# Expert lists of 96 places, weights split a whole unit at a time, and final rows scaled by three engines

## The chip, the core and the metric

The kernel runs on one core of a Trainium2 chip. Its engines run side by side, each through its own queue in order: PE (TensorE) multiplies matrices, DVE (VectorE), ACT (ScalarE) and POOL (GpSimd) work on elements, and SP starts transfers (ACT and POOL can too). The metric is the device time of one execution in microseconds (us).

## The reference, cut to what matters

A layer of a decoder: attention, cross-attention, and then a mixture of 16 experts over 512 tokens of width 1024; the change lies in the mixture and in the norm behind it. Each token takes two experts of one group.

```
    u = _rmsnorm(h, norm_ffn)                       # 512 x 1024
    expert_id, weights = two best experts of the best group of each token
    for e in range(16):
        hidden = silu(u @ w_gate[e]) * (u @ w_up[e])    # 1024 -> 256
        y = y + gate[:, e:e + 1] * (hidden @ w_down[e]) # 256 -> 1024
    h = h + y
    return _rmsnorm(h, norm_final)
```

With these inputs the experts are chosen by 44 to 95 tokens each (counted from the reference's routing).

## The kernel before

The expert stage runs over the experts e = 0 to 15. An expert's tokens stand in a list of CAP = 128 places; POOL gathers their rows into `xe` (128 x 1024), two experts ahead. PE transposes `xe` in eight 128 x 128 blocks (L130); ACT rounds a transposed half to `xh` in the matmul's short type (fp32r) and DVE subtracts that to get the rest, `xl` (L132). The weights come by SP's queue in units of 256 KB pairs, six an expert: c0 to c3 hold 256 rows of gate and up each ([128, 2, 512], 1024 elements a partition), d0 and d1 128 rows of down each. The transfers are far ahead of their use.

`esplit` makes two fp32r tiles of weights: ACT casts them to `wh` (L732), DVE subtracts to `wl` (L733). It works on half a unit, [128, 512], and turns through eight half slots (four tiles of two halves). A product of two split numbers is three matmuls (`mm3`, L137 to L139): x high by w high, x high by w low, x low by w high. The weights are the moving operand with 512 columns; the tokens are the stationary one. Per expert that makes 24 gate/up matmuls into `gu` and 9 into `dn`; the last quarter of down is one fp32 matmul of two passes (L1273), which reads `w` itself. In between stand `sg` (ACT's Silu of `gu`, L1240), DVE's product (L1242), two transposes of it (L1249), and `hh`, `hl`, `hf` from them (L1253 to L1255).

A cast overwrites a slot that an earlier cast filled, so it waits for the last matmul on the slot's old contents. In program order the split calls of an expert are c0 to c3, d0, d1; half of d1 goes through `esplit`. A scheduler puts the instructions into each engine's queue; on ACT the casts of an expert's c1 to c3 stand behind the product of the expert before (`issue_after(W["hid"])`), while the cast of c0 stands ahead of that expert's `sg`.

ACT scales `dn` by the routing weights into `y`, half by half (L1287), and SP stores `y` to a table `Y` (CAP rows an expert). For e = 14 and 15 the combination is done by matmuls with 0/1 matrices (`combine`, L1217). When expert 14 comes, POOL issues eight gathers that add rows of `Y` to `HO` (L1293), two for each of the four token tiles t, and behind them the load of the final norm's gain `g_fin` (L1303). The end ("combine") adds the matmuls' part to `HO` (L1312), squares it on ACT (L1313), takes a reciprocal root in a few small steps (L102 to L110), multiplies the rows by it and `g_fin` on DVE (L1320, two halves a tile), and stores (L1322). Tokens beyond CAP places are treated behind a branch (`overflow`).

## Time and profile before

| | us |
|---|---|
| median of 3 runs (lowest to highest) | 654.46 (653.68 to 654.64) |
| own time of the profiled execution | 653.75 |
| its span | 652.1 |
| PE busy | 609.8 (94%) |
| DVE busy | 460.8 (71%) |
| ACT busy | 375.6 (58%) |
| POOL busy | 56.8 (9%) |

The busy times are sums over the span, which holds stages with different limits. Matmuls are pipelined: one starts about 0.23 us after the other and ends some 0.39 us after its own start, so that what PE can do in a stretch is read from the distances of starts. The profiled execution took 0.7 us less than the median of the runs.

### The profile page before, as it was taken

What the parts mean: (1) busy time and instruction counts of PE and PEld (TensorE: products, weight loads), DVE (VectorE), ACT (ScalarE), POOL (GpSimd) and SP (SyncE); (2) the same over time, 40 slices, a digit from 0 to 9 for tenths busy, and PEclk for the clock granted to TensorE, in tenths of its full rate; (3) what the DMA queues carried; (4) which work ended last, traced back from release to release, by engine and by line L of the source; (5) the groups of instructions that cost most, each with busy time, mean ns of one, the idle gap of its engine ahead of it and who ended that gap; (6) DMA issues with size and microseconds to landing.
All of it is one profiled execution on the core that took longest, in us unless ns stands there. A gap on an engine that the chain in (4) does not pass through costs nothing.

```text
span 652.1 us, 10038 instructions
## 1 busy us (share of the span) xinstructions
PE 609.8 (94%) x3435; PEld 496.6 (76%) x3436; DVE 460.8 (71%) x943; ACT 375.6 (58%) x754; POOL 56.8 (9%) x87
## 2 busy tenths in 40 slices
PE   3999999999999989999999999999999999999970
PEld 2988777888786888888988898777677777777740
DVE  4843798843698996746933574458889999998944
ACT  5632567742576776415622453423388989989741
POOL 2000000000000010000000003000341101100530
PEclk9999999999999999999999999999999999999995
DMA  8545748026766446550643223984999999999593
GB/s 280 175 129 129 193 100 211 22 61 157 162 153 162 110 133 193 173 181 0 185 140 96 68 68 102 370 305 143 299 284 383 387 384 382 383 386 359 111 209 137
DMA packets 105464, 128.86 MB, mean 198 GB/s; under 512 B 8440, under 2 KB 82224, under 8 KB 105408
## 3 DMA queue, kind: packets, MB, share of 16 engines
q1 hardware_dynamic: 101088, 114.40, 55.9%
q0 software_dynamic: 4320, 13.77, 7.8%
q8 instruction: 28, 0.46, 0.3%
q14 instruction: 28, 0.23, 0.1%
HBM read 103.96 MB, written 11.56 MB: 177 GB/s over the span
## 4 chain that ended last, share of the span: by engine, by line
PE 75%; DVE 8%; DMA 7%; ACT 5%; issue 2%; POOL 1%; SPq 0%; DVEq 0%; ACTq 0%; POOLq 0%
PE pj L137 6%; PE pj L139 6%; PE pj L138 6%; PE gu L137 4%; PE pja L137 4%; PE gu L138 4%; PE gu L139 4%; PE pja L138 4%; PE pja L139 4%; PE tr L130 3%; PE pjb L138 3%; PE pjb L137 3%; PE pjb L139 3%; PE o L315 2%; PE dn L137 2%
## 5 line engine op out<-in xcount | busy, mean ns | idle before, releaser
L91 DVE TENSOR_TENSOR wl<-w,wh 128x1024 fp32r<-128x1024 f32 (+1 forms) x64 | 78.0, 1221 | 77.0 <-ACT wh L90 76.5
L90 ACT CAST wh<-w 128x1024 fp32r<-128x1024 f32 (+1 forms) x64 | 67.2, 1050 | 101.4 <-PE pj L138 33.1
L733 DVE TENSOR_TENSOR wl<-w,wh 128x512 fp32r<-128x512 f32 x168 | 108.4, 685 | 5.6 <-ACT wh L732 4.8
L732 ACT CAST wh<-w 128x512 fp32r<-128x512 f32 x168 | 96.6, 621 | 12.8 <-PE gu L139 9.8
L138 PE MATMUL pj<-ul,wh 128*128 128x512 f32 x128 | 51.6, 403 | 0.0
L137 PE MATMUL pj<-uh,wh 128*128 128x512 f32 x128 | 51.3, 401 | 0.0
L139 PE MATMUL pj<-uh,wl 128*128 128x512 f32 x128 | 51.2, 400 | 0.0
L137 PE MATMUL gu<-wh,xh 128*128 128x512 f32 x120 | 48.5, 404 | 0.2 <-ACT xh L132 0.2
L139 PE MATMUL gu<-wh,xl 128*128 128x512 f32 x120 | 47.6, 397 | 0.0
L138 PE MATMUL gu<-wl,xh 128*128 128x512 f32 x120 | 47.1, 393 | 0.0
L137 PE MATMUL pj<-wh,uh 128*128 128x256 f32 (+1 forms) x128 | 37.5, 293 | 2.2 <-ACT uh L132 2.2
L139 PE MATMUL pj<-wh,ul 128*128 128x256 f32 (+1 forms) x128 | 37.5, 293 | 0.0
L138 PE MATMUL pj<-wl,uh 128*128 128x256 f32 (+1 forms) x128 | 37.3, 292 | 0.0
L137 PE MATMUL pja<-wh,fmh 128*128 128x512 f32 x80 | 32.5, 406 | 0.0
L138 PE MATMUL pja<-wl,fmh 128*128 128x512 f32 x80 | 31.9, 399 | 0.0
L139 PE MATMUL pja<-wh,fml 128*128 128x512 f32 x80 | 31.8, 397 | 0.0
L137 PEld LDWEIGHTS pj<-uh,wh 128*128 128x128 f32 x128 | 24.1, 188 | 5.1 <-issue 0.2
L372 ACT ACTIVATE p<-lg,nm 128x512 f32<-128x512 f32 (+3 forms) x32 | 16.9, 527 | 19.0 <-DVE nm L370 18.7
L139 PEld LDWEIGHTS pj<-uh,wl 128*128 128x128 f32 x128 | 24.1, 188 | 4.8
L138 PEld LDWEIGHTS pj<-ul,wh 128*128 128x128 f32 x128 | 24.1, 188 | 4.7
L137 PEld LDWEIGHTS pj<-wh,uh 128*128 128x128 f32 x128 | 25.1, 196 | 3.0 <-ACT uh L132 2.8
L139 PEld LDWEIGHTS gu<-wh,xl 128*128 128x128 f32 x120 | 22.5, 188 | 5.3 <-issue 0.2
(356 smaller groups left out, 1618.9 us busy)
## 6 DMA issues: line engine op xcount, KB each, us to landing
w<-in_w_exp_gate_dram SPq DMA_DIRECT2D x64, 256.0 KB, 7.7
w<-in_w_exp_up_dram SPq DMA_DIRECT2D x64, 256.0 KB, 7.7
w<-in_w_exp_down_dram SPq DMA_DIRECT2D x32, 512.0 KB, 7.6
w<-in_w_in_dram SPq DMA_DIRECT2D x24, 512.0 KB, 4.6
w<-in_w_xkv_dram SPq DMA_DIRECT2D x16, 512.0 KB, 4.2
Y<-y SPq DMA_DIRECT2D x14, 512.0 KB, 8.6
KH<-th SPq DMA_DIRECT2D x32, 128.0 KB, 2.3
w<-in_w_out_dram SPq DMA_DIRECT2D x8, 512.0 KB, 5.7
```

Of the source, the lines that this page charges most:

```text
L90: nc.scalar.copy(h, raw)
L91: nc.vector.tensor_sub(l, raw, h)
L130: nc.tensor.transpose(pt[:, j, :], src[:, k * 128:(k + 1) * 128], ident)
L137: nc.tensor.matmul(o, lh, rh, start=start, stop=False)
L138: nc.tensor.matmul(o, lh, rl, start=False, stop=False)
L139: nc.tensor.matmul(o, ll, rh, start=False, stop=stop)
L315: nc.tensor.matmul(o[hh * HD:(hh + 1) * HD, i * 128:(i + w) * 128], V[:, s, vcol + hh * HD:vcol + (hh + 1) * HD], pTs[hh][:, at:at + w, :] ...
L372: nc.scalar.activation(p_[:, cs], lg[:, cs], AF.Exp, bias=nm, scale=1.0, accum_out=sm)
L732: nc.scalar.copy(h, raw)
L733: nc.vector.tensor_sub(l, raw, h)
```

## The change

Five things are edited. (1) CAP becomes 96: `xe`, `xh`, `hh`, `y` and the rows of `Y` shrink to 96 rows or columns; a transpose makes 96 columns, and matmuls with the tokens as the stationary operand use 96 of its columns, while the moving operand stays at 512. The overflow branch goes on in rounds of MORE = 128. (2) `esplit` takes a whole unit, [128, 1024], in one cast and one subtraction, and draws a tile from the rings `wh` and `wl`, four tiles each, for every call; d1 uses half of its tile. (3) The PSUM pool of `dn` has two tiles of two banks where it had four of one bank; `y` is scaled by one instruction over 1024 elements. (4) `g_fin` is loaded by SP's queue while expert 14 is issued. (5) In the end ACT squares the whole row in one instruction (not for the last tile); POOL (DVE in the last tile) multiplies the second half by `g_fin`, DVE scales the first half, ACT scales the second half by the reciprocal root.

```diff
--- before.py
+++ after.py
...
-CAP = 128
+CAP = 96
+MORE = 128
...
     NEP, NEP2 = 19, 6
...
     def esplit(raw):
-        if not halves:
-            for kind in ("wh", "wl"):
-                tiles = [wtile(kind, [2, 512], F32R) for _ in range(4)]
-                halves.append(itertools.cycle([t[:, i, :] for t in tiles for i in range(2)]))
-        h, l = (next(x) for x in halves)
-        nc.scalar.copy(h, raw)
-        nc.vector.tensor_sub(l, raw, h)
-        return h, l
+        h, l = (wtile(kind, [2, 512], F32R) for kind in ("wh", "wl"))
+        if raw.shape[-1] == 512:
+            raw = raw.unsqueeze(1) if len(raw.shape) == 2 else raw
+        else:
+            raw = raw.rearrange("p a (n c) -> p (a n) c", n=2)
+        n = raw.shape[1]
+        nc.scalar.copy(h[:, :n], raw)
+        nc.vector.tensor_sub(l[:, :n], raw, h[:, :n])
+        return [(h[:, i, :], l[:, i, :]) for i in range(n)]
...
-        xe = xp.tile([128, D], F32, name="xe", bufs=2)
-        at = idx[:, e:e + 1] if e < FIRST else lists[:, e, 0:1]
...
-    dnp = pool(ps3, "dnp", bufs=4, space=PSUM)
+    dnp = pool(ps3, "dnp", bufs=2, space=PSUM)
...
+            x.append([xp.tile([128, 4, CAP], F32R, name=n, bufs=3) for n in ("xh", "xl")])
...
+            for j in range(4):
+                k = half * 4 + j
+                nc.tensor.transpose(pt[:, j, :CAP], xes[e][:, k * 128:(k + 1) * 128], ident[:CAP, :CAP])
+            nc.scalar.copy(x[-1][0], pt[:, :, :CAP])
+            nc.vector.tensor_sub(x[-1][1], pt[:, :, :CAP], x[-1][0])
...
-        gu = gup.tile([128, 2 * FF], F32, name="gu")
+        gu = gup.tile([128, 2 * FF], F32, name="gu")[:CAP]
...
-                parts = []
-                for kk in range(2):
-                    with ExitStack() as then:
-                        if e > 1 and 2 <= c * 2 + kk < 8:
-                            then.enter_context(tc.issue_after(W["hid"].ins))
-                        parts.append(esplit(raws[n][:, kk, :]))
+                if e > 1 and c > 0:
+                    after.enter_context(tc.issue_after(W["hid"].ins))
+                parts = esplit(raws[n])
...
-        parts = [esplit(raws[n][:, 0, nh * 512:nh * 512 + 512]) for nh in range(2)]
-        part1 = esplit(raws[n + 1][:, 0, 0:512])
+        parts = esplit(raws[n])
+        part1 = esplit(raws[n + 1][:, 0, 0:512])[0]
...
-            y = xp.tile([128, D], F32, name="y", bufs=3)
-        dps = []
+            y = xp.tile([CAP, D], F32, name="y", bufs=3)
+        dp = dnp.tile([128, 2, 512], F32, name="dn")[:CAP]
...
-            dp = dnp.tile([128, 512], F32, name="dn")
...
+            mm3(dp[:, nh, :], (hh[:, 0, :], hl[:, 0, :]), parts[nh], True, False)
...
-                    for nh in range(2):
-                        nc.scalar.activation(y[:, nh * 512:nh * 512 + 512], dps[nh], AF.Copy, scale=wof(n))
+                    nc.scalar.activation(y, dp.rearrange("p n c -> p (n c)"), AF.Copy, scale=wof(n))
                 nc.sync.dma_start(Y[n * CAP:(n + 1) * CAP, :], y)
...
+            g_fin = etile([D])
+            nc.sync.dma_start(g_fin, a["norm_final"].partition_broadcast(128))
...
     mark("combine")
-    g_fin = etile([D])
-    nc.gpsimd.dma_start(g_fin, a["norm_final"].partition_broadcast(128))
...
     for t in range(NT):
+        last = t == NT - 1
...
+        cps = spread if t == 0 else dnp.tile([128, 2, 512], F32, name="dn")
+        for nh, cs in enumerate(halves):
...
+            nc.vector.tensor_add(row[:, cs], cp, row[:, cs])
+            if last:
+                nc.scalar.activation(junk[:, nh, :], row[:, cs], AF.Square, accum_out=ss[:, nh:nh + 1])
         st = small.tile([128, 1], F32, name="ss")
-        nc.vector.tensor_add(st, ss[:, 0:1], ss[:, 1:2])
+        if last:
+            nc.vector.tensor_add(st, ss[:, 0:1], ss[:, 1:2])
+        else:
+            nc.scalar.activation(junk.rearrange("p a b -> p (a b)"), row, AF.Square, accum_out=st)
...
+        ot = etile([2, 512])
+        (nc.vector if last else nc.gpsimd).tensor_mul(ot[:, 1, :], row[:, halves[1]], g_fin[:, halves[1]])
         r = rstd_of(st, D)
-        ot = etile([2, 512])
-        for nh in range(2):
-            cs = slice(nh * 512, nh * 512 + 512)
-            nc.vector.scalar_tensor_tensor(ot[:, nh, :], HO[:, t, cs], r, g_fin[:, cs],
-                                           op0=OP.mult, op1=OP.mult)
+        nc.vector.scalar_tensor_tensor(ot[:, 0, :], row[:, halves[0]], r, g_fin[:, halves[0]],
+                                       op0=OP.mult, op1=OP.mult)
+        nc.scalar.activation(ot[:, 1, :], ot[:, 1, :], AF.Copy, scale=r)
+        for nh, cs in enumerate(halves):
```

How the rows stand in the queues now is shown at three places.

PE around the end of expert e's gate/up matmuls, before. `gu` are the accumulators; L137, L138, L139 are the three matmuls of `mm3`; L1249 is the first transpose of the hidden product.

```order
L137 MATMUL gu<-wh,xh 128x512 [waits Activation_49]
L138 MATMUL gu<-wl,xh 128x512 [waits DVE_49]
L139 MATMUL gu<-wh,xl 128x512
L137 MATMUL gu<-wh,xh 128x512 [waits Activation_49]
L138 MATMUL gu<-wl,xh 128x512 [waits DVE_49]
L139 MATMUL gu<-wh,xl 128x512
L137 MATMUL gu<-wh,xh 128x512 [waits Activation_49]
L138 MATMUL gu<-wl,xh 128x512 [waits DVE_49]
L139 MATMUL gu<-wh,xl 128x512
L137 MATMUL gu<-wh,xh 128x512 [waits Activation_49]
L138 MATMUL gu<-wl,xh 128x512 [waits DVE_49]
L1249 MATMUL tr<-ident,sg 128x128 [waits DVE_49]
```
The first six rows are c3, the next five c0 of the next expert. Each half slot has its own pair of waits: one matmul waits for ACT's cast, the next for DVE's subtraction. The same place after the change (lines have moved by one or two); the first two rows are the last of c2, the next six are c3, the three after them c0 of the next expert.

```order
L139 MATMUL gu<-wl,xh 96x512
L140 MATMUL gu<-wh,xl 96x512
L138 MATMUL gu<-wh,xh 96x512 [waits Activation_49]
L139 MATMUL gu<-wl,xh 96x512 [waits DVE_49]
L140 MATMUL gu<-wh,xl 96x512
L138 MATMUL gu<-wh,xh 96x512
L139 MATMUL gu<-wl,xh 96x512
L140 MATMUL gu<-wh,xl 96x512
L138 MATMUL gu<-wh,xh 96x512 [waits Activation_49]
L139 MATMUL gu<-wl,xh 96x512 [waits DVE_49]
L140 MATMUL gu<-wh,xl 96x512
L1251 MATMUL tr<-ident,sg 128x96 [waits DVE_49]
```
There is one pair of waits to six matmuls, and three matmuls of the next c0 stand ahead of the transposes where five stood.

ACT over the same part of an expert, before, up to `sg`:

```order
L732 CAST wh<-w 128x512 [waits PE_49]
L1287 ACTIVATE y<-dn,held 128x512 [waits DMAHW1_49,PE_49]
L732 CAST wh<-w 128x512 [waits DMAHW7_49,DMAHW6_49,PE_49]
L1287 ACTIVATE y<-dn,held 128x512 [waits PE_49]
L732 CAST wh<-w 128x512
L732 CAST wh<-w 128x512 [waits DVE_49,DMAHW2_49,PE_49,Activation_49]
L132 CAST xh<-tr 128x512 [waits PE_49]
L732 CAST wh<-w 128x512 [waits DMAHW3_49,DVE_49,DMAHW4_49,PE_49,Activation_49]
L732 CAST wh<-w 128x512 [waits DVE_49,PE_49,Activation_49]
L732 CAST wh<-w 128x512 [waits DMAHW5_49,DMAHW6_49,DVE_49,PE_49]
L732 CAST wh<-w 128x512 [waits DVE_49,PE_49]
L1240 ACTIVATE sg<-gu 128x256 [waits PE_49]
```
and after: `hh` and `y` of expert e - 1, between them c2, c3 and d0 of e, then d1's half (512) of e, c0 of e + 1 and `sg` of e:

```order
L1255 CAST hh<-tr 128x192 [waits PE_49]
L1181 CAST xh<-tr 128x384 [waits PE_49]
L731 CAST wh<-w 128x1024 [waits DMAHW4_49,DMAHW5_49,DVE_49,PE_49]
L731 CAST wh<-w 128x1024 [waits DMAHW7_49,DMAHW6_49,PE_49]
L731 CAST wh<-w 128x1024 [waits DMAHW0_49,PE_49]
L1286 ACTIVATE y<-dn,held 96x1024 [waits DMAHW5_49,PE_49]
L1181 CAST xh<-tr 128x384 [waits PE_49]
L731 CAST wh<-w 128x512 [waits DMAHW1_49,DVE_49,PE_49]
L731 CAST wh<-w 128x1024 [waits DMAHW2_49,DMAHW3_49,DVE_49,PE_49]
L1242 ACTIVATE sg<-gu 96x256 [waits PE_49]
L731 CAST wh<-w 128x1024 [waits DMAHW6_49,DMAHW4_49,DVE_49]
```
Where there were single casts with `y` in two halves between them, three casts of 1024 stand in a row ahead of the whole `y`; the cast of the next expert's c0 waits for PE and stands directly ahead of `sg`. The count in that wait is that of the last matmul on this expert's c2, whose tile c0 takes over (four tiles, and c0 is the fourth call after c2); before, the two casts of c0 waited for matmuls 12 and 9 ahead of the last one of `gu`, now it is the seventh from the end, six ahead of the last. Of the three casts in a row, the first waits for c0's last matmul, the second for the last one on d1, the third for the last one on d0 of the expert before.

DVE at the end of the program, after the change: `ss` are sums of squares, `rv`, `rt`, `rr` the steps of the reciprocal root, L1314 is the last addition to `HO`, L1325 and L1327 are the multiplication by `g_fin` and the scaling of a half.

```order
L1314 TENSOR_TENSOR HO<-dn,HO 128x512 [waits PE_49]
L111 SCALAR_TENSOR_TENSOR rr_6866<-rt_6865,ry_6864 128x1 [waits DVE_49]
L1325 TENSOR_TENSOR w<-HO,w 128x512 [waits DVE_49]
L1327 SCALAR_TENSOR_TENSOR w<-HO,rr_6866,w 128x512 [waits DVE_49]
L107 SCALAR_TENSOR_TENSOR rt_6894<-ry_6893,rv_6892 128x1 [waits Activation_49]
L1319 TENSOR_TENSOR ss<-ssf 128x1 [waits Activation_49]
L111 SCALAR_TENSOR_TENSOR rr_6895<-rt_6894,ry_6893 128x1 [waits DVE_49]
L105 TENSOR_SCALAR rv_6923<-ss 128x1 [waits DVE_49]
L1327 SCALAR_TENSOR_TENSOR w<-HO,rr_6895,w 128x512 [waits DVE_49]
L107 SCALAR_TENSOR_TENSOR rt_6925<-ry_6924,rv_6923 128x1 [waits DVE_49,Activation_49]
L111 SCALAR_TENSOR_TENSOR rr_6926<-rt_6925,ry_6924 128x1 [waits DVE_49]
L1327 SCALAR_TENSOR_TENSOR w<-HO,rr_6926,w 128x512 [waits DVE_49]
```
Before the change there stood, behind its last addition (L1312):

```order
L1320 SCALAR_TENSOR_TENSOR w<-HO,rr_6875,w 128x512 [waits DVE_49]
L1320 SCALAR_TENSOR_TENSOR w<-HO,rr_6875,w 128x512
L106 SCALAR_TENSOR_TENSOR rt_6905<-ry_6904,rv_6903 128x1 [waits DVE_49,Activation_49]
L1315 TENSOR_TENSOR ss<-ssf 128x1 [waits Activation_49]
L110 SCALAR_TENSOR_TENSOR rr_6906<-rt_6905,ry_6904 128x1 [waits DVE_49]
L104 TENSOR_SCALAR rv_6934<-ss 128x1 [waits DVE_49]
L1320 SCALAR_TENSOR_TENSOR w<-HO,rr_6906,w 128x512 [waits DVE_49]
L1320 SCALAR_TENSOR_TENSOR w<-HO,rr_6906,w 128x512
L106 SCALAR_TENSOR_TENSOR rt_6936<-ry_6935,rv_6934 128x1 [waits DVE_49,Activation_49]
L110 SCALAR_TENSOR_TENSOR rr_6937<-rt_6936,ry_6935 128x1 [waits DVE_49]
L1320 SCALAR_TENSOR_TENSOR w<-HO,rr_6937,w 128x512 [waits DVE_49]
L1320 SCALAR_TENSOR_TENSOR w<-HO,rr_6937,w 128x512
```
Behind the last addition stand one L1325 and the first halves of tiles 1 to 3 (three rows of L1327), where six rows of L1320 stood.

## Rows read from the trace of the kernel before

**Rows 1.** Busy time of the engines, granted TensorE clock and DMA by stretch

```profile
core 0: us, PE busy (x) PEld busy (x) DVE busy (x) ACT busy (x) POOL busy (x), PEclk, DMA share, GB/s
500.00:520.00 20.00, 19.95 (x93) 15.28 (x92) 18.55 (x39) 17.99 (x35) 2.28 (x2) 1.00 1.06 381
606.00:610.00 4.00, 4.00 (x20) 3.26 (x19) 3.71 (x7) 3.98 (x9) 0.00 (x0) 1.00 0.32 131
634.00:638.00 4.00, 0.45 (x2) 0.03 (x1) 2.87 (x11) 2.41 (x10) 0.00 (x0) 1.00 0.44 149
```

**Rows 2.** Timeline of ACT, five of its instructions (start, duration, idle time before and releaser)

```profile
482.49 0.38 ACT L1240 ACTIVATE sg<-gu 128x256 f32<-128x256 f32 x1
...
492.36 0.39 ACT L1240 ACTIVATE sg<-gu 128x256 f32<-128x256 f32 x1
...
600.52 0.38 ACT L1240 ACTIVATE sg<-gu 128x256 f32<-128x256 f32 x1
...
603.77 1.14 ACT L732 CAST wh<-w 128x512 fp32r<-128x512 f32 x2 [0.85 <-PE gu L139]
...
605.91 0.69 ACT L1287 ACTIVATE y<-dn,held 128x512 f32<-128x512 f32 x1
```

**Rows 3.** Timeline of PE in expert 13, from the input transposes to the down projection

```profile
601.70 0.60 PE L130 MATMUL tr<-ident,xe 128*128 128x128 f32 x4
602.32 0.50 PE L137 MATMUL dn<-wh,hh 128*128 128x512 f32 x1
602.66 0.39 PE L138 MATMUL dn<-wl,hh 128*128 128x512 f32 x1
602.89 0.39 PE L137 MATMUL dn<-wh,hh 128*128 128x512 f32 x1
...
603.35 0.39 PE L139 MATMUL gu<-wh,xl 128*128 128x512 f32 x1
...
604.72 1.02 PE L1273 MATMUL dn<-w,hf 128*128 128x512 f32 x2
605.58 0.60 PE L130 MATMUL tr<-ident,xe 128*128 128x128 f32 x4
```

**Rows 4.** Instructions grouped by line and shape: count, busy us, mean ns, idle before

```profile
L732 ACT CAST wh<-w 128x512 fp32r<-128x512 f32 x168 | 96.6, 621 | 12.8 <-PE gu L139 9.8 <-PE dn L139 2.3 <-PE pja L139 0.3
L90 ACT CAST wh<-w 128x1024 fp32r<-128x1024 f32 x62 | 65.0, 1049 | 101.4 <-PE pj L138 33.1 <-PE pjb L139 19.5 <-PE pja L138 11.9
L733 DVE TENSOR_TENSOR wl<-w,wh 128x512 fp32r<-128x512 f32 x168 | 108.4, 685 | 5.6 <-ACT wh L732 4.8 <-PE gu L138 0.4
L91 DVE TENSOR_TENSOR wl<-w,wh 128x1024 fp32r<-128x1024 f32 x62 | 75.5, 1220 | 76.7 <-ACT wh L90 76.3
```

**Rows 5.** Timeline of PE at 253 us: matmuls with one moving column

```profile
253.36 1.05 PE L548 MATMUL lg<-one,sq 128*128 128x1 f32 x8
```

**Rows 6.** Timelines of SP and POOL from the last early store to the last load

```profile
606.63 0.32 SPq L1288 DMA_DIRECT2D Y<-y  x1
...
610.08 1.61 POOL L1293 DMA_INDIRECT HO<-Y,slot  x1 [22.15 <-DVE wl L733]
...
627.24 1.55 POOL L1293 DMA_INDIRECT HO<-Y,slot  x1 [3.04 <-DMA HO<-Y,slot]
628.21 1.22 POOL L1303 DMA_DIRECT2D w<-in_norm_final_dram  x1
```

**Rows 7.** Timelines of DVE and of SP after the last gather

```profile
636.57 0.69 DVE L1312 TENSOR_TENSOR HO<-dn,HO 128x512 f32<-128x512 f32 x1 [0.89 <-DMA HO<-Y,slot]
...
637.50 0.21 DVE L106 SCALAR_TENSOR_TENSOR rt<-ry,rv 128x1 f32<-128x1 f32 x1
637.84 1.41 DVE L1320 SCALAR_TENSOR_TENSOR w<-HO,rr,w 128x512 f32<-128x512 f32 x2
...
643.44 1.41 DVE L1320 SCALAR_TENSOR_TENSOR w<-HO,rr,w 128x512 f32<-128x512 f32 x2
...
644.22 1.09 SPq L1322 DMA_DIRECT2D out_dram<-w  x2
```

More of the change, by code (lines that the diff above doesn't have):

```diff
@@ L771, in layer @@
     nc.gpsimd.dma_start(Y[LATE * CAP:, :].rearrange("o (p c) -> (o p) c", p=128), zero8)
-    zeroi = rt.tile([128, NE, 2], I32, name="zeroi")
+    zeroi = rt.tile([CAP, NE, 2], I32, name="zeroi")
     nc.gpsimd.memset(zeroi, 0)
@@ L813, in layer @@
     nc.gpsimd.memset(picks[:, 1:5, :], 2.0)
-    iop = rp.tile([128, CAP], BF, name="iop")
-    nc.gpsimd.iota(iop, pattern=[[1, CAP]], base=1, channel_multiplier=0,
+    iop = rp.tile([128, 128], BF, name="iop")
+    nc.gpsimd.iota(iop, pattern=[[1, 128]], base=1, channel_multiplier=0,
                    allow_small_or_imprecise_dtypes=True)
@@ L1037, in layer @@
     xp = pool(c3, "xp", side="right")
-    xf = xp.tile([128, KT, 128], F32, name="y", bufs=3)
+    xf = xp.tile([128, KT, CAP], F32, name="y", bufs=3)
     for half in range(2):
         ks = slice(half * 4, half * 4 + 4)
-        W["xf"] = nc.vector.tensor_mul(xf[:, ks, :], xs[half],
-                                       gT[:, ks].unsqueeze(2).to_broadcast([128, 4, 128]))
+        W["xf"] = nc.vector.tensor_mul(xf[:, ks, :], xs[half][:, :, :CAP],
+                                       gT[:, ks].unsqueeze(2).to_broadcast([128, 4, CAP]))
     ps2.close()
     def overflow():
-        Y2 = dram.tile([NE * 3 * CAP, D], F32, name="Y2")
+        rounds = -(-(S - CAP) // MORE)
+        Y2 = dram.tile([NE * rounds * MORE, D], F32, name="Y2")
         P2 = dram.tile([NE * 128, NT], F32, name="P2")
@@ L1064, in overflow @@
                 nc.vector.tensor_scalar(of, pv, -float(CAP), 0.0, op0=OP.add, op1=OP.max)
-                nc.vector.scalar_tensor_tensor(of, ev, 3.0 * CAP, of, op0=OP.mult, op1=OP.add)
+                nc.vector.scalar_tensor_tensor(of, ev, float(rounds * MORE), of, op0=OP.mult, op1=OP.add)
                 oi = xo.tile([128, NT], I32, name=f"oslot{n}")
@@ L1074, in overflow @@
                 nc.sync.dma_start(pe, P2[ds(e * 128, 128), :])
-                for r in range(3):
+                for r in range(rounds):
                     n_e = nc.values_load(cnti[0:1, ds(e, 1)], min_val=0, max_val=S)
-                    rows = Y2[ds(e * 3 * CAP + r * CAP, CAP), :]
-                    with tc.If(n_e > CAP * (r + 1)) as more:
-                        ior = xo.tile([128, CAP], F32, name="ior")
-                        nc.vector.tensor_scalar(ior, iop, float(CAP * (r + 1)), None, op0=OP.add)
+                    rows = Y2[ds(e * rounds * MORE + r * MORE, MORE), :]
+                    with tc.If(n_e > CAP + MORE * r) as more:
+                        ior = xo.tile([128, MORE], F32, name="ior")
+                        nc.vector.tensor_scalar(ior, iop, float(CAP + MORE * r), None, op0=OP.add)
                         ips = ps.tile([128, 2], F32, name="ips", bufs=1)
                         for t in range(NT):
-                            oh = xo.tile([128, CAP], BF, name="ooh", bufs=2)
+                            oh = xo.tile([128, MORE], BF, name="ooh", bufs=2)
                             nc.vector.tensor_scalar(oh, ior, pe[:, t:t + 1], None, op0=OP.is_equal)
@@ L1175, in head @@
         for half in range(2):
-            x.append([xp.tile([128, 4, 128], F32R, name=n, bufs=3) for n in ("xh", "xl")])
-            to_fm(trp, xes[e][:, half * 512:half * 512 + 512], *x[-1], 0, nk=4)
+            x.append([xp.tile([128, 4, CAP], F32R, name=n, bufs=3) for n in ("xh", "xl")])
+            pt = trp.tile([128, 4, 128], F32, name="tr")
+            for j in range(4):
[3 more added lines that the diff above has]
+            nc.vector.tensor_sub(x[-1][1], pt[:, :, :CAP], x[-1][0])
         if e + 2 < NE:
@@ L1216, in combine @@
         for part in range(2):
-            nc.tensor.matmul(cp, P[:, n, t, :], ylate[n][part][:, nh, :], start=n == 0 and part == 0,
+            nc.tensor.matmul(cp, P[:CAP, n, t, :], ylate[n][part][:CAP, nh, :], start=n == 0 and part == 0,
                              stop=n == NE - LATE - 1 and part == 1)
@@ L1243, in layer @@
         if e == NE - 1:
[L1244 removed]
+            spread = dnp.tile([128, 2, 512], F32, name="dn")
             for nh in range(2):
[L1246 removed]
+                combine(spread[:, nh, :], 0, nh, 0)
         pt = trp.tile([128, 4, 128], F32, name="tr")
         for f in range(2):
[L1249 to L1255 removed]
+            nc.tensor.transpose(pt[:, f, :CAP], hid[:, f * 128:(f + 1) * 128], ident[:CAP, :CAP])
+        hh = xp.tile([128, 2, CAP], F32R, name="hh", bufs=1)
+        hl = xp.tile([128, 2, CAP], F32R, name="hl", bufs=1)
+        hf = xp.tile([128, CAP], F32, name="hf", bufs=1)
+        W["last"] = nc.scalar.copy(hh, pt[:, 0:2, :CAP])
+        nc.vector.tensor_copy(hf, pt[:, 1, :CAP])
+        nc.vector.tensor_sub(hl, pt[:, 0:2, :CAP], hh)
         n = 6 * e + 4
[L1257 to L1258 removed]
+        parts = esplit(raws[n])
+        part1 = esplit(raws[n + 1][:, 0, 0:512])[0]
         late = e >= LATE
```

58 lines of the change are left out of this document (23 added, 35 removed).

## The prediction

> **What bounds the kernel now.** First the stretches. In a full stretch of the expert stage PE is busy 19.95 of 20 us at a granted clock of 1.00, DVE 18.55, ACT 17.99; the weights come at 381 GB/s [rows 1]. Is PE or the weights the bound? At 606 to 610 us, with two experts to go, the DMA share has fallen to 0.32 while the work goes on [rows 1]: the transfers had run ahead, and PE sets the pace. ACT's timeline gives that pace: `sg` starts at 492.36 (e = 2) and 600.52 (e = 13), 108.16 us for 11 experts, **9.83 each**; the interval before was 9.87 [rows 2].
>
> Second, what one expert costs PE, from its timeline [rows 3]. Matmuls of 512 columns start .23 apart (602.66, 602.89) and end .39 after their start. Four transposes last .60 together, the end of the last included; with an end of .16 (.39 - .23) they take (.60 - .16)/4 = .11 each. The fp32 matmul takes 605.58 - 604.72 = .86. So 33 x .23 + .86 + 10 x .11 = 9.55. The rest, .28, is one wait: the transposes of 601.70 are done with issuing at 602.14, `dn` begins at 602.32 (.18), and after that pause the next start is .34 behind instead of .23 (.1).
>
> Third, the end [rows 6, 7]. `y` of expert 13 is finished at 605.91 + .69 = 606.60, stored from 606.63; 3.45 us later POOL starts the first of eight gathers, the eighth at 627.24, and behind them `g_fin`. The last gather lets DVE add at 636.57; multiplications by `g_fin` (L1320) start at 637.84, and the last of the two stores listed at 644.22 is issued at 644.98 (644.22 + 1.09 - .32 for one issue, [rows 6]). From 636.57 that is 8.4; 652.1 - 644.98 = 7.1 behind it stay. So the end of the kernel hangs on the `y` of expert 13, then on the gathers, then on DVE.
>
> **The cast of c0 becomes a loop through PE, ACT and DVE.** Let z be the start of the last matmul on c2 of expert e. It ends at z + .39, ACT hears of it .04 later (603.35 + .39 = 603.74, cast at 603.77 [rows 2, 3]) and casts the whole unit in 1.05, DVE then subtracts in 1.22 [rows 4]. With .04 to .05 a hand-over that is z + .43, z + 1.48, z + 1.52, z + 2.74, and PE's second matmul on the next c0, the one that reads `wl`, can start at z + 2.79. PE has until then only the six matmuls of c3 and the first of c0: it reaches that matmul at z + .23 x 8 = z + 1.84. **It stalls .95**, and the start after a pause costs another .1. What queues behind it: the rest of c0, the transposes of `sg`, `hh`, the down projection, so all of the next expert, whose c2 ends the loop again. The old wait goes: one more gate/up matmul (.23) now stands between the transposes and `dn`, and DVE's product with `sg` and ACT's `hh` are made during and right behind the stall. So 9.55 + .95 + .10 = **10.60** an expert, +.77 on 9.83. Before, the casts of c0 were free 12 and 9 matmuls ahead of the end of `gu`, and worked on 512 in .62 and .685 [rows 4]: the same sum, .39 + .04 + .62 + .04 + .685 + .05 = 1.83 after a release 12 matmuls (2.76) ahead, is hidden. From e = 1 to e = 13 there are 12 intervals: **+9.2** (11, if the first is still covered by early loads: +8.5). If the old .28 stays beside the stall, +3.4 more; that is the upper end.
>
> Does the larger instruction pay elsewhere? Two casts of 512 in a row take 1.14 [rows 2], one of 1024 takes 1.05: ACT gains .09 a unit. This is time on an engine that PE doesn't wait for, but at c0. The Trainium skill, "Perfetto Trace Analysis", section "Optimizing Scalar/DVE Operations", says that grouping into larger operations helps where the engine is saturated, and that where ScalarE or VectorE are not saturated but make bubbles on another engine, breaking instructions up can let work finish sooner. By the first sentence the sum would fall by 5 x .09 an expert on ACT, by the second it rises as above; the rows show ACT at 17.99 of 20, and the second carries.
>
> **96 columns give PE nothing.** The moving operand stays at 512, so the 33 matmuls stay at .23. A transpose holds `xe` as stationary operand (128 columns, now of 96 rows) and moves an identity of 96 columns instead of 128. Eight matmuls with one moving column take 1.05 together, (1.05 - .16)/8 = .11 each [rows 5], as much as a transpose with 128: the moving columns do not set it. I take 0; what fewer rows could give is a rival below. The gathers of `xe` and the stores of `Y` get a quarter smaller; both lie beside PE, but for the last store: 128 KB less at 381 GB/s, **-.3**.
>
> **`y` of expert 13.** It starts the end. Before: 606.60 - 600.52 = 6.08 behind `sg` [rows 2]. After: `sg` starts .04 behind the end of c3's last matmul, at z + 6 x .23 + .39 + .04 = z + 1.81, so the stall ends at sg + .98. Then two matmuls of c0 (.33 + .23), six transposes (.66) and one matmul (.23): `dn` begins at sg + 2.43. Twelve matmuls in a row, of which three are gate/up, take 2.76; the ninth, the last one on d1, ends at sg + 2.43 + 8 x .23 + .39 = 4.66. ACT may cast c3 then: 4.70, and d0 behind it, each at a distance of about .96 (1.05 less the overlap of .09, two casts of .62 starting .52 apart in 1.14); only then, at 6.62, comes `y` with 1024 elements, 1.11 (1.05 x .69/.62 is 1.17, 1.05 + .07 is 1.12). It ends at sg + 7.73: **+1.65**. Here the casts ahead of it, not the down projection (whose last matmul ends at 2.43 + 2.76 + 1.02 = 6.21), are late.
>
> **Gathers and end.** The eight gathers are the same rows of 4 KB and the same waits on each other: 0. `g_fin` leaves POOL's queue, where it stood behind all of them and was the last thing that the scaling waited for (637.84), and goes to SP's, behind the store of `Y`, with nothing behind it until the stores of the end: it lands some 15 us early. So tile 0 is scaled ahead of the last gather; but on DVE the additions, and the steps of tiles 1 and 2, come in turn with the rest. From the last gather G, in DVE's order: the rest of tile 2's addition .69, tile 3's first half .69, then the wait for PE, whose next four matmuls need the tile of two banks that the addition frees (.33 + 2 x .23 + .39 and hand-overs: 1.25), its addition .69, L1325 .69, L1327 of tile 1, 2 and 3 at .71 each (1.41 for two [rows 7]), between the last two the small steps of tile 3's root (two of .21 [rows 7] and one on ACT about as long: .65), two issues .38: 7.2, and some eight hand-overs of .04 make 7.5 to 7.6 where 8.4 stood: **-.9**. Its bounds: 0, if PE's matmuls at G run at half the clock (it stays 1.00 in 634 to 638 with PE busy .45 of 4 us [rows 1]); and -3.3, if nothing of tiles 1 and 2 were left at G (.69 + 1.25 + .69, a square of about .62 as ACT's cast of 512, .65, .71, .38: 5.0, with hand-overs 5.1). POOL's multiplication of 512 has no row; DVE's is .69, and even at 2 us it lies beside the gathers, which take 26.5 us for eight (610.08 to 636.57).
>
> **Sum.** 9.2 + 1.65 - .3 - .9 = +9.65; 653.75 + 9.65 = 663.4 for an execution like the profiled one, which is .7 below the median of the runs: **664**. A difference under 0.2%, about 1.3 us, is what a measurement of this kernel can't tell from none.
>
> **Rivals.** (B) *ACT becomes the bound.* ACT has 2 us of 20 free [rows 1]; if the cast of c0 does not start at its release because `y` or d1's half stand late ahead of it (.5 an expert), the loop is 11.1: 12 x .5 = +6 on top, 670. For it speaks the row of three casts. Against it: `y` ends at sg + 7.73, `xh` and d1's half bring ACT to about sg + 8.75 (.62 each, less the overlaps), and the release comes at sg + 10.60 - 1.81 + .43 = sg + 9.22, so that .5 is free; from there on each .1 more on ACT costs 1.2 us. (C) *Transposes get cheaper with 96 rows.* 10 x .11 x 32/128 = .27 an expert: 12 x .27 = 3.3 less, 660.8. Rows 5 say that the load of the stationary operand sets their .11, but there it had 128 rows. The Trainium skill, "TensorE: Matmul & The Clock Gate", section "LDWEIGHTS (loading the stationary operand)", says that a load's time goes by the columns and not by the contraction, so that 96 rows of 128 columns would cost the same; the trace before has no load of fewer rows to agree or not. (D) *Faster: no stall.* From 1.84 - .43 - .09 = 1.32 downwards for cast and subtraction together the stall is gone; then PE runs through at 9.55 with no pause of .28 either: 12 x -.28 = -3.4, `y` +.7 (the three casts stay, .95 of the 1.65 goes), store -.3, end -.9: -3.9, so 650.5. The same comes out if the tile that c0 takes is one that stood free 12 matmuls earlier. Against it: 1.05 and 1.22 are means over 62 instructions each, and the count in the wait. (E) *A list over 96.* With 95 places at most the branch is not taken; if a place more were counted, the branch's rounds would run, over 680.
>
> **How the numbers follow.** Forecast .77 (662 to 667: 11 intervals, or the old .28 beside the stall), B .08, C .06, D .08, E .01. 664 is the forecast's. Range 660 to 669: it takes in C, and of B the lower part; D and E stay outside. Faster by over 0.2% is D but for its weak cases, .06; those, a stall hidden in part, are within 0.2%: .02; slower are the rest, .92.
>
> **What would show it.** In the changed trace: `sg` 10.6 apart; a wait of about .95 of PE on DVE's `wl` (L732) once an expert, behind one matmul on `wh`; ACT's cast of c0 idle before on PE `gu`; `y` of expert 13 at sg + 7.7; first L1327 ahead of the last gather; about 7.5 us from there to the last issue. It is wrong if PE's starts run through c0 at .23, if transposes of 96 take less than .11, if the cast of c0 does not wait for PE, or if `g_fin` is late on SP.

## The result and the profile after

The changed kernel takes **664.26 us** (median of 4 runs, 663.41 to 666.26) beside 654.55 (4 runs, 653.68 to 655.54) of the kernel before on the same chip: a ratio of 1.0162 [1.0145, 1.018], slower. The forecast was 664.0. Its profiled execution took 666.26, the longest of the four, with a span of 664.6, so the two profiles lie 12.5 apart where the medians lie 9.7 apart. The readings below are from the profiles.

The page's first part gives busy us, share of the span and count of each engine. No engine but PE is near the whole span, and over 500 to 520 us PE too is busy only 18.45 of 20 us, where it was 19.95 [rows 1].

```profile
PE 612.6 (92%) x3435; PEld 481.4 (72%) x3436; DVE 451.5 (68%) x861; ACT 365.7 (55%) x662; POOL 60.3 (9%) x89
```

ACT's timeline (start, duration, idle time before and its releaser) answers to [rows 2]: `sg` of experts 1, 2 and 13, the cast of c0 ahead of the last one, and `y` of expert 13.

```profile
483.95 0.38 ACT L1242 ACTIVATE sg<-gu 96x256 f32<-96x256 f32 x1 [0.34 <-PE gu L140]
494.38 0.38 ACT L1242 ACTIVATE sg<-gu 96x256 f32<-96x256 f32 x1 [0.34 <-PE gu L140]
...
607.62 1.05 ACT L731 CAST wh<-w 128x1024 fp32r<-128x1024 f32 x1 [0.53 <-PE gu L140]
...
609.00 0.38 ACT L1242 ACTIVATE sg<-gu 96x256 f32<-96x256 f32 x1 [0.34 <-PE gu L140]
...
615.53 1.10 ACT L1286 ACTIVATE y<-dn,held 96x1024 f32<-96x1024 f32 x1
```

From 494.38 to 609.00 are 11 intervals of 10.42 us; before it was 9.83. The cast of c0 has waited for PE. What follows on PE answers to [rows 3]:

```profile
607.19 0.39 PE L140 MATMUL gu<-wh,xl 128*96 128x512 f32 x1
...
608.80 0.40 PE L138 MATMUL gu<-wh,xh 128*96 128x512 f32 x1
609.98 0.47 PE L139 MATMUL gu<-wl,xh 128*96 128x512 f32 x1 [0.78 <-DVE wl L732]
610.28 0.39 PE L140 MATMUL gu<-wh,xl 128*96 128x512 f32 x1
610.51 0.33 PE L1251 MATMUL tr<-ident,sg 96*128 96x96 f32 x2
610.68 0.49 PE L1180 MATMUL tr<-ident,xe 96*128 96x96 f32 x4
610.96 0.45 PE L138 MATMUL gu<-wh,xh 128*96 128x512 f32 x1
611.25 0.48 PE L138 MATMUL dn<-wh,hh 128*96 128x512 f32 x1
```

The matmul at 607.19 is the last on c2. It ends at 607.58, the cast starts at 607.62, DVE's subtraction at 608.70, and the second matmul on c0 can start at 609.98: 2.79 behind the start of c2's last one, as worked out. It starts 1.18 behind the first one (608.80) where .23 would do: a stall of .95. (The row shows .78 of idle time, which counts from the end of the first one, .40 behind its start.) It comes once an expert: grouped over 480 to 620 us (count, busy us, mean ns, idle time and releaser), PE's idle time ahead of L139 of `gu` is 10.1 us, all of it for `wl`, about .78 in each of 13 experts.

```profile
L139 PE MATMUL gu<-wl,xh 128*96 128x512 f32 x110 | 45.0, 409 | 10.1 <-DVE wl L732 10.1
```

At the end, POOL's first and eighth gather and SP's last issues answer to [rows 6, 7]:

```profile
620.50 1.61 POOL L1292 DMA_INDIRECT HO<-Y,slot  x1 [24.62 <-DMA w<-in_norm_final_dram]
...
636.60 1.54 POOL L1292 DMA_INDIRECT HO<-Y,slot  x1 [0.92 <-DMA HO<-Y,slot]
```

```profile
617.05 0.38 SPq L1297 DMA_DIRECT2D w<-in_norm_final_dram  x1
...
649.22 9.67 SPq L1331 DMA_DIRECT2D out_dram<-w  x8
```

`g_fin` is indeed issued early, at 617.05. Yet from the eighth gather's issue to the end of the last issue it takes 658.89 - 636.60 = 22.29, where before it took 645.31 - 627.24 = 18.07. PE and DVE show why:

```profile
635.97 0.80 PE L1219 MATMUL dn<-w 96*128 96x512 f32 x1
640.01 8.45 PE L1219 MATMUL dn<-w 96*128 96x512 f32 x22 [3.24 <-DVE HO L1314]
650.51 2.07 PE L1219 MATMUL dn<-w 96*128 96x512 f32 x4 [2.05 <-DVE HO L1314]
```

```profile
639.17 0.69 DVE L1314 TENSOR_TENSOR HO<-dn,HO 128x512 f32<-128x512 f32 x1 [4.48 <-DMA HO<-Y,slot]
...
641.40 0.69 DVE L1314 TENSOR_TENSOR HO<-dn,HO 128x512 f32<-128x512 f32 x1 [0.89 <-PE dn L1219]
643.11 0.69 DVE L1314 TENSOR_TENSOR HO<-dn,HO 128x512 f32<-128x512 f32 x1 [1.01 <-PE dn L1219]
```

PE makes six combining matmuls (four of them earlier) and then idles 3.24, until DVE's first addition is done, which waited for a gather; 22 + 4 = 26 matmuls are still to come. Before, this row stood ahead of the first addition (629.12), and 16 were left:

```profile
624.69 2.80 PE L1217 MATMUL dn<-w 128*128 128x512 f32 x11 [0.24 <-DVE w L1277]
```

After the pause PE runs at a granted clock of 0.50, the lower of its two levels, 1.2 GHz (the column behind the five engines; then DMA share and GB/s):

```profile
640.00:644.00 4.00, 3.99 (x9) 3.02 (x10) 1.90 (x3) 1.65 (x4) 1.28 (x1) 0.50 1.05 208
```

Four matmuls now take 1.7 us and the additions come 1.70 apart, each waiting for PE and no longer for a gather. So the chain that ends last runs through PE here:

```profile
640.01 6.49 PE dn L1219 x14
```

### The profile page after: what moved, and what is told of

The parts are those of the page before. It is cut to its first block, busy times and chain, and to the rows that moved or that the text cites. A ratio compares the mean times of both kernels' runs of the same rounds, so it can differ in the third digit from the quotient of the medians.

```text
span 664.6 us, 9816 instructions
## 1 busy us (share of the span) xinstructions
PE 612.6 (92%) x3435; PEld 481.4 (72%) x3436; DVE 451.5 (68%) x861; ACT 365.7 (55%) x662; POOL 60.3 (9%) x89
## 4 chain that ended last, share of the span: by engine, by line
PE 70%; DVE 12%; ACT 7%; DMA 6%; issue 2%; SPq 1%; DVEq 0%; ACTq 0%
PE pj L138 6%; PE pj L140 6%; PE pj L139 6%; PE pja L138 4%; PE pja L139 4%; PE pja L140 4%; PE gu L139 4%; DVE wl L732 3%; PE gu L140 3%; PE pjb L139 3%; PE pjb L138 3%; PE pjb L140 3%; PE gu L138 3%; ACT wh L731 3%; PE o L316 2%
## 5 line engine op out<-in xcount | busy, mean ns | idle before, releaser
L91 ACT CAST wh<-w 128x1024 fp32r<-128x1024 f32 (+1 forms) x64 | 67.2, 1050 | 101.7 <-PE pj L139 33.1
L732 DVE TENSOR_TENSOR wl<-w,wh 128x1024 fp32r<-128x1024 f32 x92 | 102.0, 1131 | 29.3 <-ACT wh L731 27.7
L731 ACT CAST wh<-w 128x1024 fp32r<-128x1024 f32 (+1 forms) x92 | 87.8, 971 | 22.2 <-PE gu L140 16.2
L139 PE MATMUL gu<-wl,xh 128*96 128x512 f32 x120 | 49.6, 413 | 10.9 <-DVE wl L732 10.9
L139 PE MATMUL pj<-ul,wh 128*128 128x512 f32 x128 | 51.6, 403 | 0.0
L138 PE MATMUL pj<-uh,wh 128*128 128x512 f32 x128 | 51.3, 400 | 0.0
L138 PE MATMUL gu<-wh,xh 128*96 128x512 f32 x120 | 48.1, 401 | 0.2 <-ACT xh L1181 0.2
L140 PE MATMUL gu<-wh,xl 128*96 128x512 f32 x120 | 47.3, 394 | 0.0
L138 PE MATMUL pj<-wh,uh 128*128 128x256 f32 (+1 forms) x128 | 37.7, 294 | 2.1 <-ACT uh L133 2.1
L139 PE MATMUL pj<-wl,uh 128*128 128x256 f32 (+1 forms) x128 | 37.5, 293 | 0.0
L139 PEld LDWEIGHTS gu<-wl,xh 128*96 128x96 f32 x120 | 19.4, 162 | 22.2 <-DVE wl L732 15.7
L138 PE MATMUL pja<-wh,fmh 128*128 128x512 f32 x80 | 32.5, 406 | 0.0
L139 PE MATMUL pja<-wl,fmh 128*128 128x512 f32 x80 | 31.9, 399 | 0.0
L138 PEld LDWEIGHTS pj<-uh,wh 128*128 128x128 f32 x128 | 24.1, 188 | 5.1 <-issue 0.2
L139 PEld LDWEIGHTS pj<-ul,wh 128*128 128x128 f32 x128 | 24.1, 188 | 4.8
L138 PEld LDWEIGHTS pj<-wh,uh 128*128 128x128 f32 x128 | 25.3, 198 | 2.9 <-ACT uh L133 2.7
L373 ACT ACTIVATE p<-lg,nm 128x512 f32<-128x512 f32 (+3 forms) x32 | 16.8, 526 | 18.7 <-DVE nm L371 18.4
```

What stands on the lines that cost most here:

```text
L91: nc.scalar.copy(h, raw)
L138: nc.tensor.matmul(o, lh, rh, start=start, stop=False)
L139: nc.tensor.matmul(o, lh, rl, start=False, stop=False)
L140: nc.tensor.matmul(o, ll, rh, start=False, stop=stop)
L373: nc.scalar.activation(p_[:, cs], lg[:, cs], AF.Exp, bias=nm, scale=1.0, accum_out=sm)
L731: nc.scalar.copy(h[:, :n], raw)
```

## Experiments

Diffs are against the changed kernel unless said otherwise. Medians stand beside those of the kernel before from the same chip.

**Half slots alone put back, whole units alone put in.** In `half_split`, `esplit` and the delay of its halves are those of the kernel before, and the rest is changed; `unit_only` is the kernel before with whole units alone.

```diff
-        h, l = (wtile(kind, [2, 512], F32R) for kind in ("wh", "wl"))
...
+        h, l = (next(x) for x in halves)
```

> The changed kernel with one edit undone: esplit works on half units again (eight half slots, as before the change); lists of 96, the dn tiles of two banks, g_fin on SP and the new end stay. Loop theory (the cast of c0 waits for c2 and stalls PE .95 an expert): the stall is gone, sg 9.6 apart instead of 10.42, y of expert 13 about 6 behind its sg instead of 7.6; 12 x .8 + 1.6 = 11 less, 653 us. Rival (the loss in the loop comes from y of 1024 and the two-bank dn tiles): sg stays above 10.2 apart, 660 us or more.

> The kernel before with one edit alone: esplit takes whole units. Lists of 128, dn tiles of one bank and the old end stay. Loop theory: sg at least 10.6 apart instead of 9.85 (transposes of 128 cost .2 more than those of 96), 12 x .75 = 9 more and 1.5 for y of expert 13: 665 us or more, with one wait of PE on wl an expert. Rival (the loss comes from the other edits): 654.5 us, sg 9.85 apart.

Measured: `half_split` 654.78 (10 runs, 652.96 to 657.13) beside 653.33, ratio 1.0017 [0.9999, 1.0036]; `unit_only` 669.45 (4 runs) beside 653.33, 1.0245 [1.0228, 1.0262]. In the profiles `sg` stands 9.42 apart in the one and 11.07 in the other, whose PE waits for `wl` in every second expert, and in the others for DVE's product with `sg` (the expectation had one wait for `wl` in each):

```profile
606.22 0.44 PE L1245 MATMUL tr<-ident,sg 128*128 128x128 f32 x2 [0.52 <-DVE sg L1238]
...
617.45 0.50 PE L138 MATMUL gu<-wl,xh 128*128 128x512 f32 x1 [1.12 <-DVE wl L732]
```

The whole units are the cost, +16.1 by themselves. The other edits give some 6 us of that back; beside half units the same edits gain nothing (`half_split`). 11.07 is also more than the 10.60 that the prediction has for whole units: the loop is longer in this kernel, as in `four_banks` below.

**Only c0 in halves.**

```diff
-        nc.scalar.copy(h[:, :n], raw)
-        nc.vector.tensor_sub(l[:, :n], raw, h[:, :n])
+        for i in ([slice(0, 1), slice(1, 2)] if first else [slice(0, n)]):
+            nc.scalar.copy(h[:, i], raw[:, i])
+            nc.vector.tensor_sub(l[:, i], raw[:, i], h[:, i])
...
-                parts = esplit(raws[n])
+                parts = esplit(raws[n], c == 0)
```

> The changed kernel with c0 alone cast and subtracted in two halves of the same tile (two casts of 512, two subtractions of 512); every other unit stays whole, and the cast still waits for the last matmul on c2. Loop theory: release to use is .43 + .62 + .04 + .69 + .05 = 1.83 against 1.84 that PE has, so the stall falls from .95 to 0 to .3, sg 9.6 to 10.2 apart, 655 to 660 us. Rival (ACT and DVE are the bound and larger instructions are cheaper): one instruction more on each makes it slower, above 664 us.

Measured: 657.09 (4 runs) beside 653.33, 1.0052 [1.0035, 1.0069]; `sg` 9.86 apart in the mean, 9.6 and 10.2 by turns. The first two matmuls on c0, and further down the second one on c1:

```profile
601.49 0.40 PE L138 MATMUL gu<-wh,xh 128*96 128x512 f32 x1
601.86 0.47 PE L139 MATMUL gu<-wl,xh 128*96 128x512 f32 x1
...
604.32 0.48 PE L139 MATMUL gu<-wl,xh 128*96 128x512 f32 x1 [0.33 <-DVE wl L733]
```

The same bytes in the same tiles, released by the same matmul: only the cast and the subtraction of c0, one unit in six, are broken up. The second matmul on c0 now starts .37 behind the first: a stall of .14 where .95 stood (and none in every second expert), and the time shrinks by 7 us. The .33 in the row is a new wait, one unit later: c1 is still whole, and in every second expert PE comes to it too early. So the loop through PE, ACT and DVE is shown, and the length of its two instructions is what it costs. The Trainium skill, "Perfetto Trace Analysis", section "Optimizing Scalar/DVE Operations", says that breaking instructions up can let work finish sooner where an unsaturated engine makes bubbles on another; this run agrees, with ACT at 15.37 and DVE at 16.41 of 20 us in the changed kernel.

**The end: order, tiles, POOL.** `tail_order` lets expert 15's subtraction (L1278), which stood behind the first addition, go ahead of it. `four_banks` gives `dn` four tiles of one bank again, with `y` in two halves. `no_pool` leaves all multiplications by `g_fin` to DVE.

```diff
+        with tc.issue_after(W["yl"].ins):
+            nc.vector.tensor_add(row[:, cs], cp, row[:, cs])
```

```diff
-    dnp = pool(ps3, "dnp", bufs=2, space=PSUM)
+    dnp = pool(ps3, "dnp", bufs=4, space=PSUM)
...
-            cp = cps[:, nh, :]
+            cp = spread[nh] if t == 0 else dnp.tile([128, 512], F32, name="dn")
```

```diff
-        (nc.vector if last else nc.gpsimd).tensor_mul(ot[:, 1, :], row[:, halves[1]], g_fin[:, halves[1]])
+        nc.vector.tensor_mul(ot[:, 1, :], row[:, halves[1]], g_fin[:, halves[1]])
```

> The changed kernel with one order on DVE: the additions to HO are issued only after the last y of expert 15 is split (L1278), which in the changed kernel stands behind the first addition and so behind a gather. Theory of the end: PE then has no pause of 3 us before the last 26 combining matmuls, runs them at the full clock and ahead of the gathers; from the last gather's landing to the last issue 8.5 us or less instead of 12.0: 660 to 661 us. Rival (the two tiles of two banks hold PE back by themselves, whatever the order): adds stay 1.7 apart, 664 us.

> The changed kernel with edit 3 undone: four dn tiles of one bank, y scaled in two halves; whole-unit split, lists of 96 and the new end stay. Theory of the end: with tiles of one bank PE makes the combining matmuls of tiles 0 and 1 right behind expert 15 at the full clock, as before the change (11 in 2.80 us), and from the last gather to the last store's issue pass 8 us or less instead of 12; 3 to 4 us less, 660 to 661 us. Rival (the end is long for POOL's multiplications and the order on DVE): the end stays 12 long, 664 us. sg stays 10.4 apart in either.

> The changed kernel with the multiplication of the second half by g_fin on DVE in all four tiles instead of on POOL in three. If POOL's 1.28 us hold DVE up (a scaling of 1.88 instead of .75 stands beside one), DVE's instructions return to .75, but DVE has three of .69 more: 0 to 1 less, 663 to 664 us. If POOL's work lies beside DVE without touching it: 1 to 2 more, 665 us or above.

Measured: `tail_order` 664.63 (4 runs) beside 653.33, 1.016 [1.0137, 1.0183]; `four_banks` 668.05 (4 runs, 664.73 to 670.66) beside 653.56, 1.0227 [1.0191, 1.0263]; `no_pool` 665.91 (4 runs), 1.0171 [1.0144, 1.0199]. From the eighth gather to the last issue the three take 20.66, 17.16 and 21.56.

Neither order nor POOL is the main cause, since 20.66 and 21.56 lie among the other kernels with tiles of two banks (below). In `tail_order` both subtractions stand ahead, and PE still waits for three additions, and its last twelve matmuls take 5.46:

```profile
648.47 5.46 PE L1219 MATMUL dn<-w 96*128 96x512 f32 x12 [0.36 <-DVE HO L1315]
```

The tile is. In `four_banks` PE gets eleven of 32 combining matmuls done ahead of its wait, seven of them in the first row, where the changed kernel has six:

```profile
638.10 2.44 PE L1219 MATMUL dn<-w 96*128 96x512 f32 x7
...
642.45 7.96 PE L1219 MATMUL dn<-w 96*128 96x512 f32 x21 [1.91 <-DVE HO L1316]
```

The chain that ends last goes through the gathers again and not through PE:

```profile
632.38 17.12 DMA HO<-Y,slot x2
```

The clock falls here too, but there is less behind it:

```profile
644.00:648.00 4.00, 4.00 (x11) 2.86 (x10) 2.50 (x5) 2.47 (x6) 2.39 (x2) 0.53 0.98 195
```

17.16 is .9 below the 18.07 of before, the size that was forecast for the end; `best_new_end` below, with the same tiles, takes 18.36, so that the agreement may be chance. Over all kernels the new end takes 20.5 to 22.3 with tiles of two banks (six kernels) and 17.2, 17.3 and 18.4 with tiles of one; the old end took 18.1 to 19.6. The total of `four_banks` did not fall all the same, where 660 to 661 was expected: `sg` stands 10.69 apart. With tiles of one bank and `y` in two halves an expert costs .27 more in the loop of the whole units, 12 x .27 = 3.2. PE and DVE show where it comes from:

```profile
613.60 0.47 PE L139 MATMUL gu<-wl,xh 128*96 128x512 f32 x1 [1.10 <-DVE wl L732]
```

```profile
611.72 1.82 DVE L732 TENSOR_TENSOR wl<-w,wh 128x512 fp32r<-128x512 f32 x2
```

DVE's row holds the subtractions of d1's half and of c0. The cast of c0 ends at 611.97, but DVE is with d1's half until about 612.3, so that PE's second matmul comes 3.10 behind the last one on c2 (610.50) and not 2.79. In the other experts PE waits .52 for the product with `sg`. `unit_only`, which also has tiles of one bank and `y` in two halves, shows the same turns. What of that is ACT's second `y` was not tried apart. The profile is that of the fastest of the four runs (664.73, against 666.26 for the changed kernel's profile); why the others take up to 6 us more stays open.

**Lists of 96 alone, and without the whole units.** `cap_only` is the kernel before with places of 96; `best_new_end` is `half_split` with the one-bank tiles of `four_banks`.

```diff
-CAP = 128
+CAP = 96
+MORE = 128
```

> The kernel before with one edit alone: lists of 96 (with overflow rounds of 128). Theory P (PE sets the pace to the end): transposes of 96 columns are .04 cheaper each, sg 9.42 apart as in the kernel with half units, 12 x .43 = 5 less: 648 to 649 us. Rival D (the weights' transfers end at about 608 whatever PE does, and the last store of Y lies behind them): sg 9.42 apart, but the first of the eight gathers still starts at 610 or later: 652 to 654 us.

> Lists of 96, g_fin on SP and the new end, but half units in esplit and four dn tiles of one bank: the change without edits 2 and 3. Loop and end theory together: sg 9.42 apart and an end of 8 or less from the last gather: .5 to 1.5 below the kernel with lists of 96 alone, and 651 to 653 us. If the new end costs by itself (POOL against DVE): 654 to 656 us.

Measured: `cap_only` 654.84 (10 runs, 651.44 to 656.33) beside 653.56, 1.0007 [0.9987, 1.0027]; `best_new_end` 653.23 (10 runs, 649.72 to 656.46), 0.9989 [0.9966, 1.0012]: no difference. Yet `sg` stands 9.40 apart in both, .43 less than before, and in `cap_only` `y` of expert 13 ends 5.63 behind `sg`. In its profile the 12 intervals are 4.2 us shorter (the first is longer than the rest). Half of that is lost ahead of the loop, where `sg` of expert 1 starts 2.2 later. The larger loss lies behind it: the first gather comes 8.02 behind `y`, where 3.48 stood before. SP issues the store that it waits for at 605.00, in time, but 1.6 behind a load of weights:

```profile
603.39 0.33 SPq L760 DMA_DIRECT2D w<-in_w_exp_down_dram  x1
...
605.00 0.34 SPq L1294 DMA_DIRECT2D Y<-y  x1
```

Before, the transfers had run ahead by then [rows 1]; here the gather starts 7.2 behind the store's issue. What slows them? The window of 500 to 520 us of `cap_only` (last column GB/s; 381 before):

```profile
500.00:520.00 20.00, 20.00 (x99) 13.66 (x98) 18.88 (x40) 18.59 (x37) 2.63 (x3) 1.00 1.07 350
```

The share of busy DMA time is as high, and fewer bytes come. What differs between the kernels there are the gathers of `xe` and the stores of `Y`, both of 96 rows, and a shorter loop.

**Gathers of 128 rows, lists of 96.** The gather fetches 128 rows again (the last 32 are token 0 and are not read), and all else stays at 96: `cap_gather128` from `cap_only`, `after_gather128` from the changed kernel, `best_gather128` from `best_new_end`; `early_gain128` is `cap_gather128` with `g_fin` on SP's queue.

```diff
-        xe = xp.tile([CAP, D], F32, name="xe", bufs=2)
-        at = idx[:CAP, e:e + 1] if e < FIRST else lists[:CAP, e, 0:1]
+        xe = xp.tile([128, D], F32, name="xe", bufs=2)
+        at = idx[:, e:e + 1] if e < FIRST else lists[:, e, 0:1]
...
-                nc.tensor.transpose(pt[:, j, :CAP], xes[e][:, k * 128:(k + 1) * 128], ident[:CAP, :CAP])
+                nc.tensor.transpose(pt[:, j, :CAP], xes[e][:CAP, k * 128:(k + 1) * 128], ident[:CAP, :CAP])
```

> Lists of 96 alone (the kernel before with edit 1), but the gather of xe fetches 128 rows as before; the 32 rows beyond the list fetch token 0 and are not used. Theory G (a gather of 96 rows slows the transfers: in the kernel with lists of 96 the rate falls to 215 to 300 GB/s for some 4 us in each expert, at the same busy share): no such dips, 380 GB/s in 500 to 520 instead of 350, the loads end before 602, the store of Y is not held up, first gather at about 608 instead of 612, 649 to 650 us. Rival (the smaller stores of Y or the faster loop cause them): dips stay, 654 to 655 us.

> The kernel with lists of 96 and gathers of 128 rows, with g_fin on SP's queue in addition (edit 4), and the old end. If the scaling waited for g_fin as it did before the change (637.84 against 636.57, 1.3 us): 0.5 to 1.3 below the kernel without it. If DVE's queue bounds the end anyway: the same time.

> As before, with the new end (edit 5) in addition: the whole change but half units, four dn tiles of one bank, and gathers of 128 rows. With tiles of one bank the new end took 17.2 from the issue of the eighth gather to the last store against 18.1 before: 0.5 to 1 below the one with early g_fin, 648 to 649 us. If POOL's multiplications cost what they save: the same.

> The changed kernel with gathers of 128 rows. Loop theory: sg stays 10.42 apart, since the loop through c0 sets the pace and the transfers have time; 663 to 665 us, perhaps with less spread. Rival (the slow transfers set the changed kernel's pace): 658 to 660 us.

Measured beside 653.18: `cap_gather128` 649.04 (6 runs), 0.9941 [0.9921, 0.9961]; `early_gain128` 647.83 (6), 0.9911 [0.9889, 0.9933]; `best_gather128` **647.15** (6), 0.9911 [0.9891, 0.993]; `after_gather128` 664.70 (5), 1.0172 [1.0149, 1.0196]. The window of `cap_gather128`:

```profile
500.00:520.00 20.00, 20.00 (x97) 13.56 (x96) 18.68 (x41) 18.57 (x38) 2.29 (x2) 1.00 1.06 383
```

383 GB/s, the first gather 3.99 behind `y`, and the spread of the runs falls from 4.9 (10 runs) to 1.8 us (6 runs): the gather of 96 rows was the brake, since stores and loop are those of `cap_only`. `best_gather128` has the lowest median, 6.0 us below the kernel before and some 17 below the changed one; its end, from the eighth gather to the last issue, is 17.25. Whether `g_fin` on SP, or the new end on top of it, gains anything beside `cap_gather128` is not decided: the intervals overlap, and `early_gain128` and `best_gather128` have the same ratio. In the changed kernel the weights don't set the pace, and 128 rows leave `sg` 10.42 apart and the time as it is, though the rate rises from 323 to 379 GB/s (last section).

## Why the prediction was right

The mechanism that makes the kernel slower was right: the cast of c0, its loop and its stall. That the time came out to .3 us is luck. The profiles lie +12.5 apart and not +9.65, the loop 2.2 below its term and the end 5.1 above it; the medians lie +9.7 apart, since the profiled execution is 2.0 above its kernel's median and that of before .8 below.

- **The cast of c0 (forecast +9.2).** The chain z + 2.79 and the stall of .95 came out to the hundredth. That too took some luck: with `y` in two halves (`unit_only`, `four_banks`) DVE comes late to c0 and the same chain takes 3.1. The 12 intervals from e = 1 to 13 add (609.00 - 483.95) - (600.52 - 482.49) = +7.0: an expert takes 10.42, not 10.60.
- **96 columns give PE nothing (forecast 0): this step failed.** The rival that transposes get cheaper held in part. Four transposes of `xe` in a row took .36 before (605.58 in [rows 3] to the next matmul) and take .28 now (610.68 to 610.96 above). The two of `sg` take .17 (610.51 to 610.68), and .22 before (601.48 to 601.70 in [rows 3]). That is .21 an expert, 2.5 over the loop, where the rival had .27. The rows of before that [rows 3] leaves out:

```profile
601.48 0.38 PE L1249 MATMUL tr<-ident,sg 128*128 128x128 f32 x2
...
605.94 0.47 PE L137 MATMUL gu<-wh,xh 128*128 128x512 f32 x1
```

  So a transpose of `xe` took .09 already before, not the .11 that I took from the row's length of .60; the sum of 9.55 was .16 too high. The rows of the loads of the stationary operand (PEld, mean ns behind the busy us) bear on what did it. Of before:

```profile
L130 PEld LDWEIGHTS tr<-ident,xe 128*128 128x128 f32 x120 | 14.3, 140 | 9.6 <-issue 4.3 <-PE dn L139 3.1 <-PE gu L1186 1.5
```

and after:

```profile
L1180 PEld LDWEIGHTS tr<-ident,xe 96*128 96x128 f32 x120 | 12.4, 140 | 10.3 <-issue 6.4 <-PE dn L140 3.5 <-DVE hl L1257 0.5
```

  The load of 96 rows of 128 columns still takes 140 ns, which speaks for the 96 moving columns as what made the transposes shorter; rows and moving columns fell together, and no run parts them. [rows 5], from which I took that moving columns don't count, gives .11 for a matmul of one column; transposes that start .07 apart show that this is no floor here. On the load itself the Trainium skill, "TensorE: Matmul & The Clock Gate", section "LDWEIGHTS (loading the stationary operand)", says that its time goes by the columns, not by the contraction. The two rows agree.
- **The old wait of .28.** It is gone in part. With the transposes at their measured distances the sum of 9.55 becomes 9.39, and the rest of an expert before is 9.83 - 9.39 = .44. In `cap_only`, without any whole unit, 9.40 is 9.83 less .21 for the transposes and less .22 of this rest, which the gate/up matmul between the transposes and `dn` now fills; the other half stays.
- **`y` of expert 13 (forecast +1.65).** 615.53 + 1.10 - 609.00 = 7.63 behind `sg`, +1.55: right, three casts of 1024 in a row and then the whole `y`.
- **The last store (-.3).** The first gather comes 3.87 behind `y`, not 3.48: +.4.
- **The end (-.9): this step failed by sign.** From the eighth gather on it is +4.2. The first L1327, forecast ahead of the last gather, starts at 647.32, 10.7 behind its issue. The working took the tile of two banks as a wait of 1.25 at one place, and PE as ready when the last gather lands. PE was not: it stops at the first addition with 26 matmuls left, and goes on at half the clock. The bound that I gave for half the clock (0) was too narrow, since the additions behind it wait for PE. With tiles of one bank (`four_banks`, `best_gather128`) the end takes 17.2. Where the gathers themselves are issued (636.60 - 620.50 against 17.16), 1.06 comes back, and behind the last issue 1.1.
- **Sum of the profiles:** up to `sg` of expert 1 +1.5, loop +7.0, `y` +1.55, store +.4, gathers -1.1, end +4.2, behind the last issue -1.1: +12.5, as the spans say. The +1.5 ahead of the loop was forecast as 0; the first intervals differ by up to 3 us between the profiles of all kernels, and their cause is not settled.
- **The rivals.** ACT had room (15.37 of 20) and did not become the bound; what the rival describes, d1's half late ahead of c0, happens on DVE in `unit_only` and `four_banks`. No stall is the case that `half_split` shows: 654.78, not 650.5. Its end takes 22.2 and its gathers have 96 rows; without both, `best_gather128` stands at 647.15.
